# Hybrid retention / HGRN2 decoder step on one core: the HGRN scan of a head spread over two projection units, four plain output chunks, and stores of split weights on the SP queue

## The chip, the cores and the metric

The kernel runs on one core of a Trainium2 chip. A core has TensorE (PE, matrix products; PEld is its weight load), VectorE (DVE), ScalarE (ACT), GpSimd (POOL) and SyncE (SP, here only an issuer of DMAs). The metric is the device time of one execution in microseconds. Three runs of the kernel before gave 1113.52, 1116.01 and 1116.64 us, so the median is 1116.01 us.

## What is computed

One decoder layer for a prompt of 2048 tokens and for 8 single decode tokens, model width 1024. Cut to what matters here:

```python
h = rmsnorm(x, norm_g)
p = h @ w_in                                   # 1024 -> 8 groups of 512 columns
rq, rk, rv, rg, hq, hf, hi, hgate = jnp.split(p, 8, axis=-1)
# retention, 4 heads of 128: rotary on rq and rk, one fixed decay per head
o_ret, s_ret_new = chunked_decay_recurrence(rq, rk, rv, log_gamma, s_ret)
o_ret = head_rmsnorm(o_ret, ret_g) * jax.nn.silu(rg)
# HGRN2, 4 heads of 128: a forget gate per token and channel
logf = jnp.logaddexp(jnp.log(lbf), jnp.log1p(-lbf) + jax.nn.log_sigmoid(hf))
kin = (1.0 - lbf) * jax.nn.sigmoid(-hf)
o_hg, s_hg_new = chunked_decay_recurrence(silu(hq), kin, hi, logf, s_hg)
o_hg = head_rmsnorm(o_hg, hg_g) * jax.nn.silu(hgate)
y = x + jnp.concatenate([o_ret, o_hg], axis=-1) @ w_out
y = rmsnorm(y, final_norm_g)
# where S_t = diag(f_t) S_{t-1} + k_t v_t^T  and  o_t = S_t^T q_t
```

Large products are done in three passes: each fp32 operand is split into a high part h (an ACT copy into the matmul's type) and a low part l (a DVE subtraction), and hh + hl + lh is summed.

## The kernel before

**Token stage.** The prompt is cut in 8 pairs of 128-token chunks. Three sets of weights are run over the 8 pairs (24 steps, `v_pair(i, after)`): values and HGRN inputs, then rq with rg, then rk with the HGRN gate. A pair is one step of a Strassen scheme with 7 products of 12 matmuls (tiles `pv{i}a`, `b`, `c`); `after[n]` holds what is emitted behind product n, and a half number means the middle of the next product. In the second set the rotated queries are transposed by `q_flip` (L427, `pqt`) and stored. In the third set the retention recurrence runs a chunk at a time beside the products: `r_flip` (`pkt`), `r_score` (`par`, `rA`), `r_update` (`pur`), `r_out` (`por`, `obr`), `r_turn` (`potr`), placed by `r_steps` (L755). New weights are split by `wg_split`, the next pair's tokens by `tok_ops` and `s_split`, at pairs 8 and 16 both at once.

**Units.** Then come 8 units, one for a head of HGRN in one half of the prompt (4 heads, 2 halves). The fill of a unit is its projection: f and q (`pjfh`, `pjqh`, L872), each in segments of four parts of 6 matmuls. In half 0 a segment has 512, 256 or 264 columns, in half 1 always 512. Beside the fill of unit i runs the scan of the head of unit i-1 (`hgrn_rec`, L1005): `scores0` (`pah`, 128 small matmuls), `scores(1)` and `scores(3)` (`plh`, 128 each), `scores3` (`plh`, 48), each of which needs k and q updated by DVE (`kh` L1040, `qth` L1043) and kept by ACT (`kepth` L1050); then the tail: `k0`, `k1` (transposes `pkh`), `u0`, `u1` (states, `puh` and `sth`), `o0`, `o1` (`poh`; ACT squares L969, POOL's power L111 and L112 for `orsh`, DVE `obh`) and `t0`, `t1` (transposes `poth`, L981). `merge` (L1301) sets where each step stands in the fill, by weights that run over one unit.

**The sides of a unit.** Splits of the tokens of the next block (`x_split`), decode steps (`d_load`, `d_mul`, `d_add`, `d_mm` with tile `pd`) and sums of w_out for the last stage (`t_load_raw`, `t_sum`, `t_spool`) are placed at times of `side_at`, counted in units. Weights of half 0 are split on chip (`w_load`) and the parts stored to DRAM (`w_kept`) by POOL, to be loaded again in half 1.

**Output.** With the scan of the last head run `PLAIN` chunks of the output product in plain form (`py`, 48 matmuls a chunk); the other chunks go in pairs by the Strassen scheme (`o_pair`, `po`, 84 matmuls a pair) with operands T1 to T4 loaded by POOL from what `t_spool` stored.

**Order.** The order on PE is that of the program text. On DVE, ACT, POOL and SP a scheduler orders instructions at build time, with `behind` tying some behind what stands before them; every engine then runs its list in order, so an instruction that waits holds all behind it. POOL computes the power of every norm and also issues DMAs; SP issues all other loads and stores.

Of the kernel before, what the change touches and what calls it, by code (L numbers as in the profile page):

```python
# [41 lines left out]
def step_kernel(ctx, tc, a, out):  # L42
# [100 lines left out]
    def w_load():  # L143
        if len(w_ready) < len(want):
# [10 lines left out]
            for t, x in zip(w_ready[-1], w_kept):  # L155
                w_stores.append((x[n], t))

    def w_next(j):
        n = w_used[0]
        assert want[n] == j  # L160
        while len(w_ready) <= n:
            w_load()
        w_used[0] += 1
        while w_stores:
            dst, t = w_stores.pop(0)
            pool.dma_start(dst, t.bitcast(F32))
        return w_ready[n]
# [259 lines left out]
    def q_flip():  # L427
        c, o = q_wait.pop()
# [326 lines left out]
    def r_steps(p):  # L755
# [7 lines left out]
        if p:  # L763
            put(0, lambda: r_load(cb, "g"))
# [4 lines left out]
        if p:  # L769
            put(0.5, lambda: r_turn(ca - 2))  # L770
        if p < N_V:
            put(3, lambda: r_load(ca, "q"), lambda: r_load(ca, "v"))
            put(3.5, lambda: r_flip(ca))
            put(4, lambda: r_load(ca, "g"))
            put(4.5, lambda: r_score(ca), lambda: r_update(ca))
            put(5.5, lambda: r_out(ca), lambda: r_load(ca + 1, "q"), lambda: r_load(ca + 1, "v"))
# [4 lines left out]
    for i in range(2, n_tok):  # L781
        after = {n: [] for n in range(7)}
        m, j = i // N_V + 1, i % N_V
        if N_V <= i < 2 * N_V:
            after[2.5] = [q_flip]
        if N_V < i <= 2 * N_V:
            after.setdefault(0.5 if i < 2 * N_V else 2, []).append(q_flip)
# [10 lines left out]
        elif i + 1 < n_tok:  # L798
# [4 lines left out]
            after[2] += [  # L803
                lambda i=i, t=tied: t(lambda: tok_ops(i + 1)), lambda i=i, t=tied: t(lambda: s_split(i + 1, 0))
            ]
            after[4] += [lambda i=i, t=tied: t(lambda: s_split(i + 1, 1))]
# [20 lines left out]
        if i >= N_V - 1 and j in (7, 0) and i < n_tok - 1:  # L827
            for n, (_, op, _) in enumerate(CHAIN):
                if (n + SPLIT_AT) // 7 == (j + 1) % N_V:
                    after[(n + SPLIT_AT) % 7] += [lambda op=op: behind(lambda: wg_split(op))]  # L830
        if i == n_tok - 1:
            after[0] += [w_load]
            after[1] += [lambda: x_alloc(0), lambda: x_raw.update({(0, kp): x_load(0, kp) for kp in range(4)})]
            for kp in range(4):
                after[3 + kp] += [lambda kp=kp: behind(lambda: x_split(0, kp, x_raw[0, kp]))]
# [16 lines left out]

    SEGS = {
# [4 lines left out]
    def seg_steps(w, half, seg, name, evac):  # L858
# [3 lines left out]
        def step(part):  # L862
            if part == 0:
                box["ps"] = ps_pj.tile([P, n], F32, tag="pj", name=f"pj{name}_{t0}")
# [68 lines left out]
    def tail_steps(half, hd, acol, qcol, vcol, kT, decay, old, eps, gcol, name, ksb, ns):  # L933
        st = pools["up"].tile([P, ns, P], F32, tag=f"st{ns}", name=f"st{name}")
        ob = {}

# [8 lines left out]
        def uu(g):  # L945
            pu = ps_lv.tile([P, 4, P], F32, tag="lv", name=f"pu{name}{g}")
            for j in range(4):
                pe.matmul(pu[:, j], ksb[g][:, j], vcol(4 * g + j), start=True, stop=True)
            for j in range(4):
                c = 4 * g + j  # L950
                dst = st[:, c % ns] if c < CH - 1 else pools["S"][hd - NH]
                src = old if c == 0 else st[:, (c - 1) % ns]
# [5 lines left out]
        def oo(g):  # L958
            po = ps_o.tile([P, 4, P], F32, tag="o", name=f"po{name}{g}")
# [806 lines left out]
```

## Time and profile before

| | before |
|---|---|
| median of three runs | 1116.01 us |
| profiled execution | 1114.73 us |
| its span, first to last instruction | 1113.0 us |
| mean granted TensorE clock | 0.979 |
| PE busy | 1051.3 us (94%) |
| DVE busy | 773.0 us (69%) |
| ACT busy | 555.1 us (50%) |
| POOL busy | 161.3 us (14%) |
| DMA moved | 248.31 MB, mean 223 GB/s |

Stages, from the first matmul of each: token stage 0 to 583 us, the 8 units 583.02 to 919.34, the last head's scan with the plain chunks 919.34 to 964.91, the Strassen output 964.91 to 1106. Busy time of PE counts pipelined matmuls with their overlapping ends, so it is no measure of lost time: a stage is read by its length against that of an undisturbed stage with the same matmuls. PEclk in a row is the granted clock of that stretch, 1.00 at full speed.

### The profile page before, as it was taken

What the parts mean: (1) busy time and instruction counts of PE and PEld (TensorE: products, weight loads), DVE (VectorE), ACT (ScalarE), POOL (GpSimd) and SP (SyncE); (2) the same over time, 40 slices, a digit from 0 to 9 for tenths busy, and PEclk for the clock granted to TensorE, in tenths of its full rate; (3) what the DMA queues carried; (4) which work ended last, traced back from release to release, by engine and by line L of the source; (5) the groups of instructions that cost most, each with busy time, mean ns of one, the idle gap of its engine ahead of it and who ended that gap; (6) DMA issues with size and microseconds to landing.
All of it is one profiled execution on the core that took longest, in us unless ns stands there. A gap on an engine that the chain in (4) does not pass through costs nothing.

```text
span 1113.0 us, 22326 instructions
## 1 busy us (share of the span) xinstructions
PE 1051.3 (94%) x8731; PEld 863.9 (78%) x8731; DVE 773.0 (69%) x1405; ACT 555.1 (50%) x1207; POOL 161.3 (14%) x276
## 2 busy tenths in 40 slices
PE   9999999899999899999998899998899889899997
PEld 7777777788778788888886788786686777678775
DVE  6777765786677866666665667576557688577776
ACT  7853436443436555555555466465445465323232
POOL 1410001000001011111112131120110211512112
PEclk9999999999999999999998899999999999899999
DMA  8688989378679855555555974477547573965652
GB/s 292 197 312 323 332 303 358 141 251 297 221 271 296 283 174 170 168 175 174 182 187 211 359 265 159 131 231 245 178 136 221 156 255 111 282 214 171 227 172 94
DMA packets 145081, 248.31 MB, mean 223 GB/s; under 512 B 10609, under 2 KB 78465, under 8 KB 144721
## 3 DMA queue, kind: packets, MB, share of 16 engines
q1 hardware_dynamic: 129120, 196.17, 53.0%
q0 software_dynamic: 15584, 50.44, 12.5%
q8 instruction: 68, 1.11, 0.4%
q14 instruction: 37, 0.30, 0.1%
q10 hardware_dynamic: 272, 0.30, 0.1%
HBM read 162.32 MB, written 84.54 MB: 222 GB/s over the span
## 4 chain that ended last, share of the span: by engine, by line
PE 68%; DMA 9%; issue 7%; DVE 7%; POOL 4%; ACT 3%; SPq 0%; POOLq 0%; DVEq 0%; ACTq 0%
PE po L332 11%; PE pjfh L872 6%; PE pjqh L872 5%; DMA xn<-in_x_prompt 2%; DMA v_dram<-vo 2%; PE pv L332 2%; DMA rq<-qt_dram 2%; PE par L702 1%; PE por L715 1%; PE pur L709 1%; PE plh L1070 1%; PE por L717 1%; POOL ms L257 1%; PE pv3a L332 1%; PE pv11a L332 1%
## 5 line engine op out<-in xcount | busy, mean ns | idle before, releaser
L872 PE MATMUL pjfh<-xh,w_h 128*128 128x512 f32 (+2 forms) x160 | 63.0, 394 | 0.0
L872 PE MATMUL pjqh<-xh,w_h 128*128 128x512 f32 (+2 forms) x160 | 61.0, 381 | 0.0
L872 PE MATMUL pjfh<-xh,w_l 128*128 128x512 f32 (+2 forms) x160 | 59.3, 370 | 1.7 <-issue 1.7
L872 PE MATMUL pjfh<-xl,w_h 128*128 128x512 f32 (+2 forms) x160 | 59.5, 372 | 0.4 <-DVE xl L116 0.4
L872 PE MATMUL pjqh<-xh,w_l 128*128 128x512 f32 (+2 forms) x160 | 57.2, 358 | 0.0
L872 PE MATMUL pjqh<-xl,w_h 128*128 128x512 f32 (+2 forms) x160 | 57.0, 357 | 0.0
L1050 ACT ACTIVATE kepth<-kh 128x1024 f32<-128x1024 f32 x24 | 25.4, 1060 | 61.8 <-DVE kh L1040 61.7
L1040 DVE TENSOR_TENSOR kh<-kh,fph 128x512 f32<-128x512 f32 x48 | 33.4, 696 | 21.2 <-PE plh L1070 19.0
L731 DVE SCALAR_TENSOR_TENSOR obr<-por,omr,rg 128x128 f32<-128x128 f32 x64 | 18.0, 345 | 37.0 <-POOL omr L729 32.7
L115 ACT ACTIVATE ab_h<-xr 128x512 fp32r<-128x512 f32 (+1 forms) x40 | 32.5, 840 | 17.8 <-DVE xr L286 16.8
L116 DVE TENSOR_TENSOR ab_l<-xr,ab_h 128x512 fp32r<-128x512 f32 (+1 forms) x40 | 37.5, 954 | 4.9 <-ACT ab_h L115 4.9
L872 PEld LDWEIGHTS pjfh<-xh,w_h 128*128 128x128 f32 x160 | 33.3, 208 | 8.8 <-issue 5.1
L969 ACT ACTIVATE jkh<-poh 128x128 f32<-128x128 f32 x64 | 17.9, 279 | 43.4 <-PE poh L965 42.1
L872 PEld LDWEIGHTS pjfh<-xh,w_l 128*128 128x128 f32 x160 | 33.1, 207 | 6.0 <-issue 1.5
L872 PEld LDWEIGHTS pjfh<-xl,w_h 128*128 128x128 f32 x160 | 33.1, 207 | 4.2 <-DVE xl L116 1.0
L872 PEld LDWEIGHTS pjqh<-xh,w_h 128*128 128x128 f32 x160 | 31.0, 194 | 5.5 <-issue 1.6
L872 PEld LDWEIGHTS pjqh<-xh,w_l 128*128 128x128 f32 x160 | 30.8, 193 | 4.5
L974 DVE SCALAR_TENSOR_TENSOR obh<-poh,orsh,v 128x128 f32<-128x128 f32 x64 | 18.1, 345 | 22.3 <-POOL orsh L112 13.7
L872 PEld LDWEIGHTS pjqh<-xl,w_h 128*128 128x128 f32 x160 | 31.1, 194 | 3.3
L286 DVE SCALAR_TENSOR_TENSOR xr<-xr,g_in,rb 128x256 f32<-128x256 f32 x64 | 26.7, 480 | 9.4 <-DMA xr<-in_x_t 4.3
L1563 DVE SCALAR_TENSOR_TENSOR xro<-xro,yms,fg 128x1024 f32<-128x1024 f32 (+1 forms) x15 | 18.1, 1213 | 21.5 <-POOL yms L112 21.5
L1043 DVE TENSOR_TENSOR qth<-qth,fph 128x512 f32<-128x512 f32 x48 | 32.8, 683 | 0.0
(1913 smaller groups left out, 3461.6 us busy)
## 6 DMA issues: line engine op xcount, KB each, us to landing
xr<-a_dram SPq DMA_DIRECT2D x24, 512.0 KB
S<-s_dram SPq DMA_DIRECT2D x24, 512.0 KB
xn<-in_x_prompt SPq DMA_DIRECT2D x32, 256.0 KB
xr<-in_x_t SPq DMA_DIRECT2D x16, 512.0 KB
a_dram<-xr SPq DMA_DIRECT2D x16, 512.0 KB
s_dram<-S SPq DMA_DIRECT2D x16, 512.0 KB
wgr<-in_w SPq DMA_DIRECT2D x16, 512.0 KB
xr<-a_dram SPq DMA_DIRECT2D x32, 256.0 KB
```

The source lines that it names most:

```text
L115: act.activation(h, src, AF.Copy)
L116: dve.tensor_tensor(l, src, h.bitcast(F32), op=ALU.subtract)
L286: dve.scalar_tensor_tensor(r[:, k], r[:, k], g_in[:, kk : kk + 1], spread_to[i], op0=ALU.mult, op1=ALU.mult)
L332: pe.matmul(ps, xx, ww, start=(first and n == 0), stop=(last and n == 2), skip_group_check=more)
L731: dve.scalar_tensor_tensor(o[:, cc], po[:, h], ms[:, h : h + 1], rb_of[c, "g"][:, cc], op0=ALU.mult, op1=ALU.mult)
L872: pe.matmul(ps, ww[:, kk], x[:, k, b0 : b0 + n], start=(k == 0 and i == 0), stop=(k == KT - 1 and i == 2),)
L969: act.activation(jk, po[:, j], AF.Square, accum_out=ms[:, j : j + 1])
L974: dve.scalar_tensor_tensor(ob[g][:, j], po[:, j], rs[:, j : j + 1], gcol(4 * g + j), op0=ALU.mult, op1=ALU.mult)
L1040: dve.tensor_tensor(kv[:, :, 0, :], kv[:, :, 0, :], two[:, :, 1:2].to_broadcast([P, nb, b]), op=ALU.mult)
L1043: dve.tensor_tensor(qv[:, :, 1, :], qv[:, :, 1, :], two[:, :, 0:1].to_broadcast([P, nb, b]), op=ALU.mult)
L1050: act.activation(ss[:, 512:], k[:, :HALF], AF.Copy)
L1563: dve.scalar_tensor_tensor(xro[c][:, cc], xro[c][:, cc], ms[:, 0:1], fg[:, cc], op0=ALU.mult, op1=ALU.mult)
```

## The change

1. **Scan of a head over two units.** `hgrn_rec` gives two lists. The scores and `k0`, `k1` (`levels`) run beside the next unit, at 0.08, 0.3, 0.52, 0.74, 0.93 and 0.96 of its fill; the states, outputs and transposes (`rest`) run beside the unit after that, at 0.02 to 0.7. The decays are copied to a tile of their own (`dec`, one DVE copy of 8 columns a head).
2. **Four plain chunks** in place of two (`PLAIN`): 96 plain matmuls more, one Strassen pair of 84 fewer. The last stage carries the rest of the last but one head and the whole of the last.
3. **DMAs from POOL to SP.** 52 DMAs: the 16 stores of split weights, the 16 stores of w_out sums (`t_store`, apart from the split and later) and the 20 loads of T1 to T4.
4. **Longer first unit.** The first four parts of unit 1 are run in unit 0 (`HEADED`, in a bank of another PSUM pool), and the last chunk of retention is spread over them.
5. **Flips later.** The transposes of rotated queries come one to three products later, oldest first; in pair 16 the retention steps come half a product later and the first `r_out` goes to pair 17; splits at pairs 8 and 16 come later, the splits of the first block of tokens one product earlier.
6. Decode products `d_mm` and the loads for w_out sums get other times.

```diff
+        while w_stores and w_stores[0][0] <= n:
+            _, dst, t = w_stores.pop(0)
+            sp.dma_start(dst, t.bitcast(F32))
...
-        c, o = q_wait.pop()
+        c, o = q_wait.pop(0)
...
+            d = 0 if p else 0.5
+            put(3.5 + d, lambda: r_flip(ca))
...
-            after[2.5] = [q_flip]
+            after[3.5 if i > N_V + 1 else 4.5 if i > N_V else 5.5] = [q_flip]
...
+            late = 2 if same(i) else 0
+            after[2 + late] += [
...
-                after[3 + kp] += [lambda kp=kp: behind(lambda: x_split(0, kp, x_raw[0, kp]))]
+                after[2 + kp] += [lambda kp=kp: behind(lambda: x_split(0, kp, x_raw[0, kp]))]
...
+                pl, tag = (ps_lv, "lv") if name == HEADED and t0 == 0 else (ps_pj, "pj")
...
-        steps = [(1.0, scores0), (2.3, lambda: scores(1)), (0, load), (2.3, lambda: scores(3)), (2.3, scores3)]
...
+        levels = [(0.08, scores0), (0.3, lambda: scores(1)), (0.4, load), (0.52, lambda: scores(3)),
+                  (0.74, scores3), (0.93, t["k0"]), (0.96, t["k1"])]
+        rest = [(0.02, begin), (0.12, t["u0"]), (0.24, t["u1"]), (0.36, t["o0"]), (0.44, t["o1"]),
+                (0.6, t["t0"]), (0.7, t["t1"]), (0.7, last)]
...
+    def t_store(k, n):
+        for x, y in zip("hl", tspl[k, n]):
+            sp.dma_start(t_dram[x, n][:, :, k], y.bitcast(F32).rearrange("p (a b) -> p a b", a=2))
...
-        merge(fill, rec)
-        rec = hgrn_rec(*order[i], u)
+        merge(fill, levels, late)
+        late = rest
+        levels, rest = hgrn_rec(*order[i], u)
...
-            pool.dma_start(t, t_dram[x, pair[0]][:, pair[1]])
+            sp.dma_start(t.bitcast(F32), t_dram[x, pair[0]][:, pair[1]])
...
-    PLAIN = 2
+    PLAIN = 4
...
-    merge(fill, rec, 0.95)
+    merge(fill, [(0.57 * at, f) for at, f in levels], [(0.57 * at, f) for at, f in late], [(0.55 + 0.5 * at, f) for at, f in rest])
```

Three places show how rows moved. The names in them: `x_h` and `x_l` are parts of a split operand, a number at the end of a name is a buffer.

On PE, at the scores of head 2 of half 0 (`pah`, in unit 3), before:

```order
L872 MATMUL pjfh_0_6920<-xh_5157,w_l 128x512
L1089 MATMUL pah_6936<-qh_6521,kh_6520 32x32 x32
L1070 MATMUL pah_6936<-qth_6522,kh_6520 32x16 x32
L872 MATMUL pjfh_0_6920<-xh_5157,w_h 128x512
L872 MATMUL pjfh_0_6920<-xl_5158,w_h 128x512
```

and after:

```order
L879 MATMUL pjfh_0_6858<-xh_5116,w_l 128x512
L1104 MATMUL pah_6874<-qh_6391,kh_6390 32x32 x32
L1085 MATMUL pah_6874<-qth_6392,kh_6390 32x16 x32
L960 MATMUL puh_6959<-v_6542,ksh_6830 128x128 x4
L879 MATMUL pjfh_0_6858<-xh_5116,w_h 128x512
L879 MATMUL pjfh_0_6858<-xl_5117,w_h 128x512
```

The states `puh` of the head before now follow the first scores. From `pah` to the next burst of scores (`plh`) stood 12 projection matmuls; now 18 stand there and both groups of `puh`. On the whole the four bursts of a unit are 22% of its fill apart, where they were 14%.

On POOL, at the norm of the head before the last (`orsh`, in unit 7), before, with loads of operand T2 among them:

```order
L1424 DMA oT2l_9990<-t_draml_5378 128x512
L111 TENSOR_SCALAR orsh_9673<-omsh_9664 128x4
L112 TENSOR_TENSOR orsh_9673<-orsh_9673,mhalf 128x4
L1424 DMA oT2l_9991<-t_draml_5378 128x512
L1424 DMA oT2l_9992<-t_draml_5378 128x512
L111 TENSOR_SCALAR orsh_9699<-omsh_9690 128x4
L112 TENSOR_TENSOR orsh_9699<-orsh_9699,mhalf 128x4
```

and after, at the norm in the same unit:

```order
L1157 DMA out_new_hgrn_prompt<-S_5579 128x128
L111 TENSOR_SCALAR orsh_9369<-omsh_9360 128x4
L112 TENSOR_TENSOR orsh_9369<-orsh_9369,mhalf 128x4
L111 TENSOR_SCALAR orsh_9417<-omsh_9408 128x4
L112 TENSOR_TENSOR orsh_9417<-orsh_9417,mhalf 128x4
```

No DMA stands between the two norms any more. The loads stand on SP, in the same unit, among loads of w_out (`wor`) and of outputs (`or`):

```order
L1453 DMA oT2h_10264<-t_dramh_5376 128x512
L1240 DMA out_new_hgrn_sample<-dS_9117 128x8x128
L1392 DMA wor_9624<-in_w_out 128x1024
L1453 DMA oT2h_10265<-t_dramh_5376 128x512
L1453 DMA oT2h_10266<-t_dramh_5376 128x512
L1392 DMA wor_9647<-in_w_out 128x1024
L1481 DMA or_9670<-o_dram 128x8x128
L1481 DMA or_9676<-o_dram 128x8x128
```

A load of T2 that waits for its buffer now holds the loads of `wor` and `or` behind it.

115 lines of the change are left out of this document (62 added, 53 removed).

## The prediction

> **What bounds the kernel now.** I read the page first, then the granted clock and busy time by stretch, the waits of PE, and the timeline at the longest of them.
>
> ```profile
> span 1113.0 us, 22326 instructions
> PE 1051.3 (94%) x8731; PEld 863.9 (78%) x8731; DVE 773.0 (69%) x1405; ACT 555.1 (50%) x1207; POOL 161.3 (14%) x276
> q1 hardware_dynamic: 129120, 196.17, 53.0%
> q0 software_dynamic: 15584, 50.44, 12.5%
> q8 instruction: 68, 1.11, 0.4%
> ```
>
> PE is the bound, but 94% hides how much it loses, because overlapping matmuls count as busy. So I compare stretches with equal work. The next fence has one row for unit 0, one for each of units 1 to 7, and one for the last head's scan with the plain chunks; its columns are the length, the busy time of PE, PEld, DVE, ACT and POOL with their instructions, the granted clock (PEclk), the DMA share and GB/s.
>
> ```profile
> 583.02:621.34 38.32, 33.42 (x189) 28.85 (x188) 21.57 (x45) 19.34 (x51) 7.30 (x12) 0.87 0.70 245
> 621.34:666.93 45.59, 39.97 (x641) 35.45 (x639) 31.55 (x68) 24.99 (x54) 12.11 (x18) 0.93 0.86 309
> 666.93:703.71 36.78, 36.25 (x640) 32.53 (x640) 26.59 (x64) 23.18 (x52) 8.79 (x14) 1.00 0.43 161
> 703.71:747.13 43.42, 38.60 (x639) 33.90 (x640) 27.79 (x55) 24.86 (x54) 7.26 (x10) 0.94 0.55 175
> 747.13:790.83 43.70, 39.43 (x600) 31.68 (x600) 29.38 (x66) 23.00 (x48) 3.01 (x6) 0.94 0.70 224
> 790.83:834.46 43.63, 39.35 (x609) 30.84 (x610) 24.80 (x53) 19.80 (x45) 4.08 (x7) 0.96 0.52 158
> 834.46:877.34 42.88, 39.05 (x617) 30.54 (x618) 29.08 (x57) 20.08 (x46) 5.80 (x10) 1.00 0.76 228
> 877.34:919.34 42.00, 37.84 (x610) 30.24 (x610) 33.86 (x61) 25.64 (x51) 6.35 (x11) 1.00 0.59 191
> 919.34:964.91 45.57, 39.12 (x594) 31.34 (x594) 32.46 (x58) 23.78 (x52) 13.20 (x24) 0.92 0.55 166
> ```
>
> Unit 2 (666.93) took 36.78 us at full clock; the others, with nearly the same matmuls, took 42.0 to 45.6. No engine is full in them (DVE at most 33.86 of 42.00). So a unit costs 36.8 us and the rest is waiting. Units 4 to 7 also hold 1, 2, 3 and 2 decode products. The timeline of PE (start, length, work, and in brackets the idle time before it) prices them at 0.57 us each (855.01 to 855.58), and four small products of 128 columns at 0.38 (198.33 to 198.71).
>
> ```profile
> 194.80 0.39 PE L332 MATMUL pv8c<-T1h,s71l 128*128 128x512 f32 x1
> 198.33 0.63 PE L431 MATMUL pqt<-ident,vo 128*128 128x128 f32 x4 [3.13 <-DVE vo L354]
> 198.71 0.48 PE L332 MATMUL pv8c<-T1h,s71h 128*128 128x512 f32 x1
> ...
> 855.01 0.64 PE L563 MATMUL pd<-dS,dqp 128*32 128x256 f32 x8
> 855.58 0.50 PE L872 MATMUL pjqh<-xh,w_h 128*128 128x512 f32 x1
> ```
>
> Loss in unit 1 is then 8.8; in units 2 to 7 it is 0, 6.6, 6.3, 5.7, 4.4 and 4.0, together 27.0. For unit 0 and the last stretch I need prices of long matmuls, from the chain of waits, where a run of PE without a wait stands as one piece (start, length, count):
>
> ```profile
> 667.17 2.79 PE pjfh L872 x12
> ...
> 675.36 3.02 PE pjfh L872 x24
> ...
> 679.66 3.11 PE pjfh L872 x24
> ...
> 1072.68 32.92 PE po L332 x144
> ```
>
> They give 0.2325 us for 512 columns, 0.126 and 0.130 for 256 and 264, 0.2286 in the output stage. The fill of unit 2 is 48 of each of the first three, 23.4 us, so the scan of a head is 13.4 us of PE. Unit 0 has that fill and 44 small products, 4.2 us: it loses 10.7. The last stretch has 96 x 0.2286 = 21.9 and one scan: it loses 10.3. **From 583 to 965 us, 57 us are lost**, and these are where the change works.
>
> What they are lost to, by the waits of PE (total, times, longest) and the places:
>
> ```profile
> PE poth L981 <- DVE obh L974: 12.8, 10, 2.3
> PE plh L1070 <- issue: 8.4, 4, 3.3
> PE plh L1070 <- ACT kepth L1051: 5.0, 3, 3.9
> PE potr L740 <- DVE obr L731: 4.5, 2, 2.5
> PE pqt L431 <- DVE vo L354: 3.1, 1, 3.1
> PE pjfh L872 <- issue: 1.7, 2, 1.1
> ...
> PE pkt L694 <- DVE rk L354: 1.6, 1, 1.6
> PE por L715 <- DVE rA L704: 1.7, 1, 1.7
> ```
>
> A wait is dear, since the clock falls behind it: after the 3.1 us before `pqt`, the stretch of this row (columns as above) ran at 0.51 for 3.5 us, which costs 1.7 more.
>
> ```profile
> 199.50:203.00 3.50, 3.50 (x10) 2.73 (x9) 3.50 (x4) 2.12 (x4) 0.00 (x0) 0.51 0.64 186
> ```
>
> The timelines of PE, DVE and POOL at four waits:
>
> ```profile
> 587.95 1.15 PE L740 MATMUL potr<-ident,obr 128*128 128x128 f32 x4 [1.97 <-DVE obr L731]
> ...
> 628.24 1.22 DVE L116 TENSOR_TENSOR w_l<-wr,w_h 128x1024 fp32r<-128x1024 f32 x1 [3.41 <-ACT w_h L115]
> ...
> 711.45 0.39 PE L1070 MATMUL plh<-qth,kh 128*32 128x16 f32 x25
> 713.95 0.51 PE L1070 MATMUL plh<-qth,kh 128*32 128x16 f32 x37 [2.12 <-issue]
> ...
> 916.13 0.53 POOL L1424 DMA_DIRECT2D oT2l<-t_draml  x1 [0.99 <-DVE obh L974]
> 916.73 0.19 POOL L111 TENSOR_SCALAR orsh<-omsh 128x4 f32<-128x4 f32 x1
> ```
>
> At 711.45 PE stops in the middle of a burst with nothing awaited. The 17462 PE instructions over 68 packets of the instruction queue are 257 a packet of 16 KB, so I read this as PE's next block of program not yet there: a burst of 128 small matmuls with their loads is a whole block, and two bursts stood 12 matmuls (2.8 us) apart. At 628.24 DVE stood 3.41 us for a weight that had not landed, and the scan's updates behind it. At 916.13 POOL held the norm behind a load of T2 that waited for `obh`.
>
> **The change, part by part.**
>
> *Scan over two units.* No matmul is added; a copy of 8 columns a head is nothing on DVE. The output chain (ACT squares, POOL, DVE `obh`) before `poth` had an eighth of a fill, 2.9 us, and gets 24 to 26%, 5.6 us and more; its longest wait was 2.3, so all ten should go. The bursts get 22% of 23.4, 5.1 us, and 0.8 of `puh`, 5.9 in place of 14%, 3.3. The wait at 713.95 was 2.1, so it is covered, unless a block ends just at a burst's start; then spacing does not help. DVE, ACT and POOL do the same work in fewer us: unit 7 has 33.86 us of DVE in some 38, 89%. So I leave in units 2 to 7 one stall like 713.95 with its slow clock (2.1 + 1.7) for every two units, 11 us, and take 27.0 - 11 = **-16.0**. Bounds: nothing gained, or all 27.0.
>
> *Unit 1.* The fourth weight is asked for ahead of the eight loads of values instead of behind four of them, and the first burst gets 12 x 0.126 + 24 x 0.130 = 4.6 us in place of 2.8. But DMA was 0.86 busy there, and with no rest beside it the later bursts stay close. Half: **-4.4**, between 0 and -8.8.
>
> *Unit 0.* The first `potr` stands behind the same matmuls, so its 2.0 and the slow clock stay. The second gets 24 matmuls where it had 6, 4.2 us more against its 2.5: the wait goes, and the slow clock that followed, of which I count 3.4 us (the row's 0.87 of 38.32 is 5.0 us in all, less 1.7 for the first). Against it, the parts of the next block are now split closer to their use: four DVE subtractions of 1.2 (the length at 628.24) against six matmuls of 0.126 each, a new wait of 1.2. **-4.7**, between 0 and -9.
>
> *Last stretch.* 192 plain matmuls stand beside one and a half scans. DVE gets two more chunks, and each chunk must leave its bank before the next but one; I halve the loss: **-5.2**, between +2 (a DVE wait of 2.3, as the longest of `poth`, at three chunk ends, with the old loss kept in part) and -10.3. The stage as a whole does 96 matmuls more and 84 fewer: 12 x 0.2286 = **+2.7**, on PE for certain.
>
> *Flips.* `pqt` of pair 8 comes three products, 36 matmuls or 8.2 us, later against a wait of 3.1; wait and slow clock go, **-4.8**. `pkt` and `por` of pair 16 wait 3.3; DVE is behind there, and the move of half a product (1.4) and of `r_out` should take most: **-2.0**, between 0 and -3.3.
>
> *52 DMAs from POOL to SP.* On POOL, a store or load before a norm goes (916.13); its gain is in the `poth` row already. On SP the stores wait for a split that PE needs at the same time, so I cost them at nothing; what hides them is that weights are loaded a whole unit ahead. If that cover is gone, each late weight costs what unit 1 shows, below. They are 24 MB (16 + 16 of 0.5, 16 of 0.25, 4 of 1) of q0's 50.44 MB: q1 gets them.
>
> A rule that speaks against this: the Trainium skill, "DMA: Bandwidth & Descriptors", section "Queues, rings and completion order", says each DMA engine takes turns between the queues that have work, a packet at a time. By that the 24 MB had turns of their own on q0 and would now stand in line with the loads on q1; the sum would get the price of the slow rival below.
>
> Another: "Runtime: NRT & Kernel Launch", section "Instruction fetch mechanics", in the Trainium skill, calls the cost of crossing a block of 256 instructions mostly hidden. The 257 a packet agree with the block; the 2.12 at 713.95 does not look hidden. By the rule the issue waits would have another cause, spacing would not touch them, and the sum would be that of the first rival.
>
> Sum: -16.0 - 4.4 - 4.7 - 5.2 + 2.7 - 4.8 - 2.0 = -34.4. The profiled execution took 1114.73 us, 1.3 below the median 1116.01, so 1114.7 - 34.4 = **1080 us**.
>
> **Rivals.** *The bursts still starve.* If issue waits come from DMA traffic alone, spacing gains nothing: the 10.1 us of the two issue rows stay, with the slow clock of units 3 to 5 (0.94, 0.94, 0.96 of some 43.5: 6.9) and the 4.4 of unit 1, less some 6 of the 11 already left: +15, **1095**. For it: DMA moved 160 to 309 GB/s in these units. Against: unit 6, at 228 GB/s, kept a clock of 1.00.
>
> *Nearly all goes.* If units 2 to 7 keep 1 us each (6 for 11), units 1 and the last stretch 2 each (4 for 9.5), pair 16 nothing (for 1.3) and unit 0 only its first wait with the slow clock (3.7 for 6.0), it is 14 less: **1066**. Against: DVE at 89%.
>
> *Slower: weights late on SP.* SP works in order, and a store that waits for its split, or a load of T2 or T1 that waits for its buffer, holds the next weight. Unit 1 gives the price of one late weight: 8.8 us. Half 0 has 8 weights, half 1 loads 8 again. With four late, all the 34 are gone; with six, it is 1080 + 53 = **1133**. For it: DMA 0.86 busy in unit 1, where most stores fall. Against: weights are needed about every 18 us.
>
> **How the numbers follow.** My forecast, 1071 to 1089, has 0.50; starving bursts 0.22; nearly all gone 0.16; late weights 0.12, of which 0.02 end within 0.3% (3.3 us, about what a measurement of this kernel can tell from no change) and 0.10 above. So faster 0.88, same 0.02, slower 0.10. The range takes the forecast and the larger part of both neighbours: 1060 to 1100.
>
> **What would show it.** `poth` should leave the list of waits; units 2 to 7 should take 37 to 40 us each at a clock of 0.97 or more; `pqt` should have no wait and 199 to 203 no slow clock; the last stretch should take 43.9 + 20 + 5 = 69 us. I am wrong if a group of `w_h` or `w_l` on a DMA, or new waits of PE for DVE, take more than 10 us in the units, or if waits of `plh` on issue stay above 8 us.

## The result and the profile after

The changed kernel took 1087.61 us, the median of four runs (1085.89 to 1091.66), against 1116.33 for the kernel before in the same session: a ratio of 0.975, 95% interval 0.9715 to 0.9784. The profiled execution took 1087.88 us, 26.9 less than the 1114.73 of before; the forecast was 34.4 less.

The head of the page, engines and queues:

```profile
span 1086.1 us, 22296 instructions
PE 1043.2 (96%) x8743; PEld 860.5 (79%) x8743; DVE 760.8 (70%) x1400; ACT 553.3 (51%) x1204; POOL 127.9 (12%) x224
...
q1 hardware_dynamic: 139424, 221.34, 61.5%
q0 software_dynamic: 7328, 25.27, 6.6%
q8 instruction: 69, 1.13, 0.4%
```

POOL lost its 52 DMAs (276 to 224 instructions), and q0's 50.44 MB became 25.27. The waits of PE (total, times, longest):

```profile
PE plh L1085 <- issue: 10.7, 4, 4.1
PE pkt L694 <- DVE rk L354: 3.1, 2, 2.2
PE prs L273 <- DVE dg L268: 2.5, 2, 2.1
...
PE plh L1130 <- issue: 1.9, 1, 1.9
...
PE pqt L431 <- DVE vo L354: 0.3, 1, 0.3
```

`poth` (12.8 before) and `potr` (4.5) are gone, and `pqt` fell from 3.1 to 0.3. Stops on issue inside the score bursts (`plh`) did not fall: 10.7 and 1.9, together 12.6, against 8.4 before. With the stops at other matmuls PE stood 13.0 us on issue, against 10.1 before.

The stretches, from one head's `pah` to the next, then the one behind `pqt` (length, busy time of PE, PEld, DVE, ACT and POOL, granted clock, DMA share, GB/s). The first row is unit 0, the second unit 1 without its first four parts, then units 2 to 7 and the beginning of the last stretch:

```profile
579.92:618.11 38.19, 35.62 (x226) 31.25 (x224) 19.21 (x44) 18.95 (x47) 4.83 (x7) 1.00 0.70 234
618.11:650.74 32.63, 27.60 (x562) 24.26 (x561) 26.43 (x53) 19.72 (x34) 0.00 (x0) 0.95 0.86 301
650.74:691.26 40.52, 37.95 (x639) 33.88 (x638) 30.07 (x69) 25.93 (x55) 3.61 (x6) 0.96 0.66 223
691.26:735.00 43.74, 37.74 (x640) 33.91 (x639) 27.12 (x64) 23.19 (x52) 3.59 (x6) 0.96 0.78 248
735.00:773.31 38.31, 36.49 (x600) 30.07 (x599) 27.28 (x56) 22.72 (x48) 4.33 (x6) 1.00 0.70 204
773.31:810.16 36.85, 36.85 (x607) 30.09 (x606) 24.25 (x52) 19.15 (x45) 3.59 (x6) 1.00 0.75 217
810.16:849.07 38.91, 38.34 (x618) 30.74 (x617) 28.89 (x57) 19.77 (x46) 5.78 (x7) 1.00 0.64 200
849.07:890.05 40.98, 38.62 (x609) 31.46 (x608) 33.67 (x61) 27.46 (x54) 6.48 (x9) 0.96 0.62 194
890.05:923.00 32.95, 28.64 (x510) 24.14 (x510) 23.42 (x46) 13.47 (x32) 4.92 (x9) 0.90 0.43 136
...
199.50:203.00 3.50, 3.50 (x19) 2.68 (x18) 3.47 (x5) 3.33 (x7) 0.00 (x0) 1.00 0.32 120
```

Unit 5 (773.31) has two decode products of 0.57, so an undisturbed unit of half 1 is 35.7 us. That agrees with its fill, 96 x 0.2325 = 22.3 in place of 23.4.

To compare stages whose borders moved, I priced every matmul at the interval that follows it in undisturbed runs (0.227 us for 512 columns, 0.118 and 0.121 for 256 and 264, 0.0143 for a small score) and summed what lies above. A slow clock is in these losses too:

| stage | lost before | lost after | change | forecast |
|---|---|---|---|---|
| 186 to 215 us (`pqt` of pair 8) | 6.5 | 2.2 | -4.3 | -4.8 |
| 354 to 383 us (pair 16) | 4.1 | 2.0 | -2.1 | -2.0 |
| rest of the token stage | 17.0 | 20.0 | +3.0 | 0 |
| unit 0 | 11.2 | 4.1 | -7.1 | -4.7 |
| unit 1 | 9.3 | 6.4 | -2.9 | -4.4 |
| units 2 to 7 | 32.7 | 18.9 | -13.8 | -16.0 |
| last scans and output | 11.6 | 9.1 | -2.5 | -5.2 |
| 12 more matmuls | | | +2.7 | +2.7 |
| sum | | | -27.0 | -34.4 |

The longest waits left in the units have one cause. The timeline of PE in unit 3, then the DMA of the 6.6 us ahead of the fetch of the next block of program, and of the 1.2 us that hold it (packets, MB, share of 16 engines):

```profile
699.40 0.65 PE L1085 MATMUL plh<-qth,kh 128*32 128x16 f32 x56
704.19 0.30 PE L1085 MATMUL plh<-qth,kh 128*32 128x16 f32 x6 [4.14 <-issue]
```

```profile
q1 hardware_dynamic: 620, 2.17, 90.5%
q14 instruction: 1, 0.01, 0.5%
```

```profile
q1 hardware_dynamic: 128, 0.40, 93.5%
q8 instruction: 1, 0.02, 6.1%
```

PE stopped at 700.05 with six matmuls of the burst to go. Until 701.7 the engines were 90% busy with q1 and no block of PE's program (q8, 16 KB) came; one came then, and PE went on at 704.19. A block is about 256 instructions (17622 records of PE, weight loads included, over 69 packets), so its borders can be placed by counting these records in the order of their start. In the traces of both kernels and of the twelve versions below there are 68 stops on issue of 0.6 us or more. Each stands 193 or 194 records past a multiple of 256, whatever the matmul is there, and at each PE goes on 1.2 to 1.6 us after the last packet of q8 has ended. So these stops are borders of blocks that came late.

In the units of the changed kernel a packet starts 0.9 to 1.1 us after PE enters the block before the one it brings where the DMA engines stand idle, and mostly 1.5 to 5 us, at most 7.6, after where they are busy. A block that is one burst lasts 1.2 us; in the long matmuls of the token stage a block lasts 20 us and more, and there no stop of this kind occurs. The experiments test the border and the traffic.

### The profile page after: what moved, and what is told of

The parts are those of the page before. It is cut to its first block, busy times and chain, and to the rows that moved or that the text cites. A ratio compares the mean times of both kernels' runs of the same rounds, so it can differ in the third digit from the quotient of the medians.

```text
span 1086.1 us, 22296 instructions
## 1 busy us (share of the span) xinstructions
PE 1043.2 (96%) x8743; PEld 860.5 (79%) x8743; DVE 760.8 (70%) x1400; ACT 553.3 (51%) x1204; POOL 127.9 (12%) x224
## 2 busy tenths in 40 slices
DMA packets 147130, 248.34 MB, mean 229 GB/s; under 512 B 10608, under 2 KB 78464, under 8 KB 146768
## 3 DMA queue, kind: packets, MB, share of 16 engines
q0 software_dynamic: 7328, 25.27, 6.6%
q8 instruction: 69, 1.13, 0.4%
## 4 chain that ended last, share of the span: by engine, by line
PE 65%; DMA 13%; DVE 8%; ACT 7%; issue 4%; POOL 2%; SPq 1%; DVEq 0%; POOLq 0%; ACTq 0%
PE po L332 11%; PE pjfh L879 5%; PE pjqh L879 5%; DMA xn<-in_x_prompt 4%; PE py L1502 4%; DMA qt_dram<-qt 2%; PE par L702 1%; PE plh L1085 1%; PE pur L709 1%; PE por L715 1%; PE puh L960 1%; DMA wr<-in_w_in 1%; PE poh L976 1%; PE por L717 1%; DMA wg1B<-in_w 1%
## 5 line engine op out<-in xcount | busy, mean ns | idle before, releaser
L879 PE MATMUL pjfh<-xh,w_h 128*128 128x512 f32 (+2 forms) x160 | 59.9, 374 | 0.0
L879 PE MATMUL pjfh<-xh,w_l 128*128 128x512 f32 (+2 forms) x160 | 57.0, 356 | 0.7 <-DVE w_l L116 0.7
L879 PE MATMUL pjfh<-xl,w_h 128*128 128x512 f32 (+2 forms) x160 | 57.2, 357 | 0.4 <-DVE xl L116 0.3
L1065 ACT ACTIVATE kepth<-kh 128x1024 f32<-128x1024 f32 x24 | 25.4, 1060 | 62.0 <-DVE kh L1055 58.2
L115 ACT ACTIVATE ab_h<-xr 128x512 fp32r<-128x512 f32 (+1 forms) x40 | 32.3, 840 | 17.1 <-DVE xr L286 17.0
L879 PEld LDWEIGHTS pjfh<-xh,w_l 128*128 128x128 f32 x160 | 30.8, 192 | 5.9 <-DVE w_l L116 1.6
L879 PEld LDWEIGHTS pjfh<-xh,w_h 128*128 128x128 f32 x160 | 30.6, 191 | 5.5 <-issue 1.2
L879 PEld LDWEIGHTS pjfh<-xl,w_h 128*128 128x128 f32 x160 | 30.8, 193 | 4.3 <-DVE xl L116 1.0
L742 ACT ACTIVATE obr<-potr,pk 128x128 f32<-128x128 f32 x64 | 19.0, 368 | 21.7 <-PE potr L740 21.7
L1592 DVE SCALAR_TENSOR_TENSOR xro<-xro,yms,fg 128x1024 f32<-128x1024 f32 (+1 forms) x13 | 15.5, 1202 | 18.5 <-POOL yms L112 18.5
```

The lines of the kernel that those rows point to most:

```text
L115: act.activation(h, src, AF.Copy)
L742: act.activation(o[:, cc], pt[:, h], AF.Copy, scale=ng[:, h : h + 1])
L879: pe.matmul(ps, ww[:, kk], x[:, k, b0 : b0 + n], start=(k == 0 and i == 0), stop=(k == KT - 1 and i == 2),)
L1065: act.activation(ss[:, 512:], k[:, :HALF], AF.Copy)
```

## The experiments

Each is the changed kernel but for its diff, of which the main lines are shown; the last two stand on half bursts. "The changed kernel" is 1087.61 us, ratio 0.975 (0.9715 to 0.9784); every ratio is to the kernel before, run beside it.

**The scan back in one unit.**

```diff
-        merge(fill, levels, late)
-        late = rest
+        merge(fill, levels, rest)
...
-        levels = [(0.08, scores0), (0.3, lambda: scores(1)), (0.4, load), (0.52, lambda: scores(3)),
+        levels = [(0.063, scores0), (0.207, lambda: scores(1)), (0.207, load), (0.352, lambda: scores(3)),
...
-    merge(fill, [(0.57 * at, f) for at, f in levels], [(0.57 * at, f) for at, f in late], [(0.55 + 0.5 * at, f) for at, f in rest])
+    merge(fill, levels, rest)
```

> The changed kernel with one part undone: the states, outputs and transposes of a head's scan stand again in the unit of its scores, at the places of the kernel before; all else is as changed. Theory (the spread is what brought the gain in the units): units 1 to 7 and the last stretch lose again what they lost before, less what the other parts saved, 14 to 20 us more than the changed kernel's 1087.6, so 1102 to 1108, and waits of poth on obh come back with 8 us or more. Rival (the gain in the units came from the stores on SP and the later side work): within 4 us of 1087.6, and poth below 3 us.

1104.88 us, ratio 0.9911 (0.988 to 0.9943): 17.3 us slower. Units 2 to 7 lost 36.0 in place of 18.9, unit 1 11.8 in place of 6.4, the last stage 2.6 less than the changed kernel. The waits of PE:

```profile
PE poth L994 <- DVE obh L987: 10.5, 8, 4.3
PE plh L1085 <- issue: 10.0, 8, 2.3
```

The waits of `poth` came back, as the first theory had it. The stops on issue in `plh` are about as long as with the spread, in more and shorter pieces. With 4.3 us at `pjfh` they are 15.2 us in all against 13.0: the spread did little for them.

**All 52 DMAs on POOL again.**

```diff
-            sp.dma_start(dst, t.bitcast(F32))
+            pool.dma_start(dst, t.bitcast(F32))
...
-            sp.dma_start(t.bitcast(F32), t_dram[x, pair[0]][:, pair[1]])
+            pool.dma_start(t.bitcast(F32), t_dram[x, pair[0]][:, pair[1]])
```

> The changed kernel with the 52 DMAs issued by POOL again, at their new places in the program. Theory (their queue is worth nothing to PE): within 3 us of 1087.6; POOL busy about 160 us in place of 128, q0 at 50 MB. Rival 1 (the DMAs on POOL hold the norms behind them): 5 to 8 us slower, with waits on orsh or of poth on obh of 5 us or more. Rival 2 (stores with turns of their own let the loads through): 4 us or more faster, because stalls of plh on issue or waits of DVE for weights shrink. A rule of the Trainium skill, 'DMA: Bandwidth & Descriptors', section 'Queues, rings and completion order', that a DMA engine takes turns between its queues, would give rival 2.

1103.59 us, ratio 0.990 (0.9871 to 0.9929): 16.0 us slower, more than either of the first two had it. The traced execution, 1097.68 us, is the fastest of nine; it began unit 0 4.3 us earlier than that of the changed kernel. In it the last stage lost 20.1 in place of 9.1, at one place. The wait of PE, and the timeline of POOL there:

```profile
PE poth L994 <- DVE obh L987: 9.1, 1, 9.1
```

```profile
949.14 0.39 POOL L111 TENSOR_SCALAR orsh<-omsh 128x4 f32<-128x4 f32 x1
958.34 0.81 POOL L1447 DMA_DIRECT2D woh<-t_dramh  x1 [8.82 <-issue]
959.18 1.04 POOL L112 TENSOR_TENSOR orsh<-orsh,mhalf 128x4 f32<-128x4 f32 x1
```

The second of two loads of T4 into the tiles of w_out stood 8.8 us on POOL between the two halves of one norm; DVE's `obh` and then PE's `poth` stood behind it. What the load waited for the profile does not show (`<-issue`); the load of `wol` ahead of it, issued at 948.29, took 9.7 us to land, that is until 958.0.

**Only the 32 stores on POOL**, the loads of T1 to T4 on SP.

```diff
-            sp.dma_start(dst, t.bitcast(F32))
+            pool.dma_start(dst, t.bitcast(F32))
...
-            sp.dma_start(t_dram[x, n][:, :, k], y.bitcast(F32).rearrange("p (a b) -> p a b", a=2))
+            pool.dma_start(t_dram[x, n][:, :, k], y.bitcast(F32).rearrange("p (a b) -> p a b", a=2))
```

> The changed kernel with the 32 stores issued by POOL again, the 20 loads of T1 to T4 left on SP. Theory (of the 16 us that all 52 on POOL cost, a load of T2 or T4 that waits for its buffer held the norm of the last head, 9 us at one place; stores wait for nothing long): within 4 us of 1087.6, and no wait of poth on obh above 2 us. Rival (the stores hold norms too, one by one): 5 to 10 us slower, without a long wait in the last stretch. A third way (stores with turns of their own let weights through, the rule on queues of the Trainium skill, 'DMA: Bandwidth & Descriptors', section 'Queues, rings and completion order'): 4 us or more faster.

1093.22 us, ratio 0.979 (0.9767 to 0.9813), 5.6 us slower by the medians, with intervals that overlap. No wait of `poth` remained, and the last stage lost 8.9. So by the medians about 10 of the 16 us are the 20 loads, through the norm above. For the rest there is the trace of the slowest of the four (1097.91 us): units 1 and 3 lost 11.2 and 13.8 in place of 6.4 and 7.3, by waits for `qth`, `fxh` and `w_l` and slower clocks; which store causes them stays open. The third way, a gain from queues that take turns, did not come.

**Flips back.**

```diff
-        c, o = q_wait.pop(0)
+        c, o = q_wait.pop()
...
-            after[3.5 if i > N_V + 1 else 4.5 if i > N_V else 5.5] = [q_flip]
+            after[2.5] = [q_flip]
...
-            after.setdefault(2.5 if i < N_V + 3 else 1.5 if i < 2 * N_V else 2, []).append(q_flip)
+            after.setdefault(0.5 if i < 2 * N_V else 2, []).append(q_flip)
```

> The changed kernel with the transposes of rotated queries at their old places and latest first; the retention steps of pair 16 stay as changed. Theory (the prediction's term of 4.8): the wait of pqt comes back with some 3 us at pair 8, the stretch of 29 us there loses 4 us more, and the time is 3 to 6 us above the changed kernel's 1087.6. Rival (the wait only moves: DVE is behind there and the split of the next pair's tokens takes its place): the stretch loses within 1 us of the 2.2 it loses now, and the time within 2 us.

1091.71 us, ratio 0.9784 (0.9763 to 0.9804): 4.1 slower by the medians, with intervals that overlap. The wait of PE and the stretch behind it, which is the row of before once more:

```profile
PE pqt L431 <- DVE vo L354: 4.6, 3, 3.7
```

```profile
199.50:203.00 3.50, 3.50 (x10) 2.80 (x9) 1.40 (x2) 1.09 (x2) 0.00 (x0) 0.50 0.51 142
```

From 186 to 215 us 7.4 were lost in place of 2.2. The term of 4.8 is borne out in this stretch, slow clock included.

**Two plain chunks.**

```diff
-    PLAIN = 4
+    PLAIN = 2
```

> The changed kernel with two plain chunks instead of four beside the last scans. Theory (the prediction's balance of 2.7 more matmul time against 5.2 less loss): the matmuls of the stage take 2.7 us less, but one and a half scans stand beside half as many fills, bursts and the output chain of the last head have no cover, and the stage loses 8 us or more over the changed kernel's 8.4; the time is 3 to 10 us above 1087.6. Rival (the tail spreads as well over two chunks): 1 to 4 us faster than the changed kernel, the 2.7 us of matmuls saved.

1091.70 us, ratio 0.9792 (0.9754 to 0.983): 4.1 slower by the medians, with intervals that overlap. The last stage lost 16.6 in place of 9.1, 7.5 more, with waits of `plh` for `sth` (3.2) and `poth` for `obh` (2.8); less the 2.7 of matmuls that makes 4.8. By this trace four chunks are worth it because the spread scan needs a cover there.

**The first unit as before.**

```diff
-    HEADED = "fh01"
+    HEADED = None
...
-            next_unit = unit(1)
-            early += [f for w, f in next_unit[0][:4]]
-            del next_unit[0][:4]
...
-                if n in (0, 1, 3, 5, 7, 11):
+                if n in (0, 1, 2, 4, 6, 7):
```

> The changed kernel without the longer first unit: the first four parts of unit 1 stand in unit 1 again, and the last chunk of retention is spread over 8 parts. Theory (the prediction's term of 4.7 for unit 0, read as 7 from the trace of the changed kernel): a second wait of 2 us or more for obr or rk in unit 0 comes back with a slow clock, unit 0 and unit 1 together lose 3 to 7 us more than the 10.5 they lose now, time 1090 to 1095. Rival (unit 1, the busiest for DMA, is eased when it keeps its four parts): what unit 0 loses unit 1 gains, the time within 3 us of 1087.6.

1088.23 us, ratio 0.9749 (0.9705 to 0.9792): no difference. Unit 0 lost 7.4 in place of 4.1, with a wait of `potr` for `obr` of 2.4, and unit 1 lost 4.0 in place of 6.4, as the rival had it. The longer unit moves a loss of 3 us from one unit to the next.

**Bursts cut in two.**

```diff
-        def scores(li):
-            pl = ps_lv.tile([P, 2, CH, 16], F32, tag="lv", name=f"pl{name}{li}")
+        def scoresa(li):
+            pl = box["pl"] = ps_lv.tile([P, 2, CH, 16], F32, tag="lv", name=f"pl{name}{li}")
             small(pl[:, 0], li, box["kept"])
+
+        def scores(li):
+            pl = box["pl"]
             small(pl[:, 1], li + 1)
...
+        levels = [(0.08, scores0a), (0.13, scores0), (0.3, lambda: scoresa(1)), (0.36, lambda: scores(1)), (0.4, load),
+                  (0.53, lambda: scoresa(3)), (0.59, lambda: scores(3)), (0.76, scores3),
```

> The changed kernel with each burst of 128 score matmuls cut in two of 64, a step of 6 projection matmuls or more between them; the same matmuls. Theory (PE outruns the fetch of its program, one block of 256 instructions ahead, and the fetch waits behind DMA traffic): a block then lasts longer at the bursts, and the waits on issue of plh, 12.6 us in the changed kernel, fall to 3 to 8; the time falls by 3 to 9 us, to 1079 to 1085. Rival (the fetch waits so long behind traffic that a few us more a block don't help): issue waits stay between 10 and 15 and the time within 3 us of 1087.6.

1084.37 us, ratio 0.9726 (0.9679 to 0.9773): 3.2 less by the medians, which the intervals do not tell from the changed kernel. The stops halved:

```profile
PE plh L1085 <- issue: 6.1, 3, 3.2
PE plh L1142 <- DVE qth L1058: 3.4, 1, 3.4
...
PE plh L1137 <- ACT kepth L1066: 3.1, 1, 3.1
```

Two new waits in unit 1, for DVE's update of `qth` and ACT's copy `kepth`, which now have less room, took back half of it: the unit lost 9.8 in place of 6.4.

**Less DMA traffic: no stores of split weights**, each weight read whole and split again in half 1.

```diff
-            if n >= 2 * NH:
+            if False:
...
-                w_stores.append((n, x[n], t))
+                pass
```

> The changed kernel without the 16 stores of split weights; in half 1 each weight is loaded whole once more (0.5 MB in place of two parts of 0.5 MB) and split again on ACT and DVE. 8 MB of stores leave units 0 to 3, 4 MB of loads leave units 4 to 7; DVE gets 8 subtractions of 1.2 us in units 4 to 7. Theory (fetches wait behind DMA traffic): fetches in units 0 to 3 start sooner, stalls on issue there (about 12 us of loss at 625, 635, 638, 660 and 700) halve, and the time falls by 3 to 8 us, to 1080 to 1085. Rival (the stores lie in gaps of the traffic, and DVE is the tighter engine): no fewer stalls on issue, new waits for w_l in half 1, 1088 to 1095.

1092.98 us, ratio 0.982 (0.9771 to 0.9869): 5.4 slower by the medians, with intervals that overlap a little. The traced execution, 1087.62 us, is the fastest of the four; it began unit 0 4.9 us earlier than that of the changed kernel and lost that again. DMA moved 235.74 MB in place of 248.34, and yet the stops on issue that were 10.7 are 13.0, and unit 3 lost 11.8 in place of 7.3. So fewer bytes on the whole did not help; the theory in that form fell. What stayed the same is the place. The timeline of PE with its stop, here and with the 32 stores on POOL, two programs with other traffic and the same order on PE as the changed kernel:

```profile
695.68 0.30 PE L1085 MATMUL plh<-qth,kh 128*32 128x16 f32 x6 [5.50 <-issue]
```

```profile
711.10 0.30 PE L1085 MATMUL plh<-qth,kh 128*32 128x16 f32 x6 [4.01 <-issue]
```

Three times PE stops with six of the burst to go. That fits the border of a block, and just as well a fault of the burst itself. The next two runs separate these.

**64 matmuls more in the warm-up.**

```diff
-    for n in range(14):
-        pe.matmul(wu, ones, ones, start=True, stop=True)
+    for n in range(14 + 64):
+        pe.matmul(wu[:, :16] if n > 13 else wu, ones, ones[:, :16] if n > 13 else ones, start=True, stop=True)
```

> The changed kernel with 64 matmuls of 16 columns more in the warm-up at the start, 128 instructions or half a block of program, while PE still waits for its first operands; nothing else is changed. Theory (PE stops where a block of its program ends while a fetch waits behind traffic): the stops on issue move to other matmuls or change in length by 1 us or more each, and their sum lies between 6 and 18 us against 12.6; the time lies within 5 us of 1087.6. Rival (the stops come from the bursts themselves, a bank of PSUM or an operand): the same bursts stop at the same matmul for the same time, within 0.5 us.

1111.2 us, ratio 0.9962 (0.9942 to 0.9983): 23.6 slower, outside both. The groups of instructions on PE show why (busy, mean ns of one):

```profile
L84 PE MATMUL wu<-ones 128*128 128x16 f32 x128 | 24.9, 352 | 0.0
L84 PE MATMUL wu<-ones 128*128 128x128 f32 x28 | 5.6, 391 | 1.1 <-POOL ones L78 1.1
```

The first product of the token stage began at 31.33 us in place of 6.96: the added work was on the path. And such a matmul stands twice in the trace (64 as 128, as 14 stand as 28), with its weight load each time: 256 instructions, a whole block (the page has 70 packets of instructions in place of 69). So the borders of blocks did not move in the program, and the stops stayed: 4.1 us in unit 3 and 3.8 in the last stretch, where the changed kernel has 4.3 and 3.8 by the same pricing. The five stops of over 1 us in the changed kernel stand at the same matmuls again, with 20, 10, 6, 7 and 21 of their burst to go. The run tells the theories apart no further.

**Half a block more, behind unit 0.** The first head's first scores do one group twice.

```diff
             small(p0, 0)
+            if half == 0 and "n" not in pools:
+                pools["n"] = small(p0, 0)
             update(0)
```

> The changed kernel with one group of 64 small matmuls of the first scores (first head of half 0) done twice, into the same bank: 128 instructions, half a block, and under 1 us more before everything behind it; the warm-up is left alone. Theory (PE stops where a block ends while the next is not fetched): behind that place blocks end half a block earlier in the program, so the stops on issue of units 2 and 3 and of the last stretch (2.0, 4.3 and 3.8 us in the changed kernel) come at other matmuls of the burst, at least two of the three differ by 1 us or more in length, and the time lies 0 to 8 us off 1087.6 on either side. Rival (the stops belong to the burst: a bank, an operand or the clock): each of the three stops stands at the same matmul of its burst with the same length within 0.5 us, as they did with a whole block more.

1082.75 us, ratio 0.9709 (0.9673 to 0.9745): 4.9 less than the changed kernel by the medians, with more work and intervals that overlap a little. In the changed kernel the stops of unit 2 and of the last stretch, beside the one at 704.19, are these:

```profile
661.95 0.27 PE L1085 MATMUL plh<-qth,kh 128*32 128x16 f32 x10 [1.84 <-issue]
...
904.53 0.51 PE L1085 MATMUL plh<-qth,kh 128*32 128x16 f32 x21 [3.65 <-issue]
```

With the shift, units 1 to 4 and the stretch behind the last `pah`, then stops in bursts of units 1 and 4:

```profile
614.18:651.61 37.43, 28.38 (x626) 25.20 (x625) 28.84 (x59) 20.51 (x35) 0.00 (x0) 0.95 0.81 288
651.61:688.18 36.57, 36.09 (x639) 32.39 (x638) 27.80 (x63) 24.85 (x54) 3.61 (x6) 1.00 0.63 220
688.18:726.16 37.98, 36.34 (x639) 32.74 (x638) 27.13 (x64) 23.21 (x52) 3.60 (x6) 1.00 0.87 286
726.16:771.01 44.85, 38.35 (x600) 31.52 (x599) 27.33 (x56) 22.88 (x48) 5.39 (x6) 0.96 0.57 174
888.75:921.70 32.95, 32.28 (x575) 27.06 (x575) 27.06 (x53) 17.57 (x42) 6.07 (x11) 1.00 0.48 151
```

```profile
625.38 0.32 PE L1085 MATMUL plh<-qth,kh 128*32 128x16 f32 x15 [2.04 <-issue]
...
632.62 0.46 PE L1085 MATMUL plh<-qth,kh 128*32 128x16 f32 x34 [1.65 <-issue]
...
727.90 0.49 PE L1085 MATMUL pah<-qth,kh 128*32 128x16 f32 x35 [0.75 <-issue]
...
752.79 0.24 PE L1085 MATMUL plh<-qth,kh 128*32 128x16 f32 x4 [3.62 <-issue]
```

Unit 2 took 36.57 us and unit 3 37.98, in place of 40.52 and 43.74: their stops of 2.0 and 4.3 (by the pricing above) are gone, and so is the 3.8 of the last stretch, whose clock here is 1.00 where it was 0.90 and whose loss fell from 9.1 to 3.3. But in unit 4, whose longest stop was 1.0, one of 3.6 appeared, and the unit took 44.85 us in place of 38.31; unit 1 has stops of 2.0, 1.7 and 1.3 where it had one of 1.9. DMA was busier in unit 3 than in the changed kernel (0.87, 0.78). So the same bursts beside as much traffic stop or don't by where the program's blocks end.

The stops moved more than they shrank: PE stood 11.6 us on issue in all, against 13.0. Units 1 to 7 together took 274.57 us (614.18 to 888.75), against 271.94 (618.11 to 890.05) in the changed kernel. Of the 7.1 us by which the traced span is shorter, 5.8 lie in the last stretch and the output, and 3.9 ahead of the added group, where every engine runs the same instructions in the same order; 2.6 were lost in the units between. How much of the 4.9 the shift is worth stays open.

**Half bursts, w_out sums moved**, in two ways.

```diff
-    for k, at in enumerate((0.4, 1.0, 1.8, 2.5)):
+    for k, at in enumerate((0.4, 1.0, 1.8, 4.45)):
```

> The kernel with half bursts, and the fourth group of w_out sums (its loads, sums and 2 MB of stores) moved from units 2 and 3 to units 4 and 5, away from the ten loads of the next block of tokens. Theory (fetches wait behind the traffic of that place): the stop in the scores of unit 3, 4.3 us in the changed kernel and 2.5 with half bursts, falls under 1 us, unit 3 loses 2 to 4 us less, and the time is 1078 to 1083. Rival (what holds the fetch is the loads of tokens, whatever else runs): the stop stays above 2 us, and the time is that of half bursts, 1084.4, or more, since units 4 and 5 get the work.

1083.31 us, ratio 0.9705 (0.9683 to 0.9726), 4.3 under the changed kernel by the medians, with intervals that overlap a little. The stop of unit 3 went: the unit lost 0.2 in place of 7.3, and stops on issue of `plh` fell to 2.9. Half bursts alone, with the same order on PE and so the same borders, lost 4.3 there, so the traffic of that place does matter. Unit 5 lost 3.2 in place of 0.1, by a wait for `kept` (2.1).

```diff
-    for k, at in enumerate((0.4, 1.0, 1.8, 2.5)):
+    for k, at in enumerate((0.4, 1.4, 2.2, 3.7)):
```

> Half bursts with the second, third and fourth group of w_out sums moved to where no late update and no load of tokens stands beside them (1.4, 2.2 and 3.7 in place of 1.0, 1.8 and 2.5). Theory: unit 1 loses 4 to 7 us in place of 9.8 with half bursts, unit 3 under 2 in place of 4.3, and the time is 1075 to 1081, below both kernels. Rival (the waits of DVE in unit 1 come from weights that land late, not from the sums): unit 1 loses 9 or more still, and the time is 1081 to 1086, as with the other half-burst kernels.

1088.04 us, ratio 0.9765 (0.9726 to 0.9804): neither. Unit 1 lost 4.8 in place of 9.8 with half bursts, as the theory had it, but one wait in unit 4 took it back. The waits of PE, and the issues of SP ahead of it:

```profile
PE pjqh L879 <- DMA w_h<-w_kepth: 9.4, 1, 9.4
```

```profile
729.31 0.52 SPq L1210 DMA_DIRECT2D t_dramh<-wos30h  x1
...
732.50 0.51 SPq L1210 DMA_DIRECT2D t_draml<-wos31l  x1
...
734.19 2.02 SPq L179 DMA_DIRECT2D xr<-a_dram  x2
736.32 1.14 SPq L149 DMA_DIRECT2D w_h<-w_kepth  x1
```

The four stores waited 5.2 us on SP for their splits ahead of the weight, which was then asked for at 736.32, and PE stood 9.4 us for it. They were not alone: ahead of them SP had waited 6.4 us for DVE with a load of tokens, and 2.1 with one of a decode state.

## Why the prediction was right, and where it was off

The forecast was faster, 1080 us in 1060 to 1100; it was faster, 1087.6.

*Scan over two units (-16.0).* Right in mechanism and close in size: -13.8, and +17.1 in these units when undone. `poth` left the list, as said. The part on the bursts failed: "so it is covered" did not hold for stops like that at 713.95: in all, those in the scores came to 12.6, more than the 8.4 before. The exception that stood beside it, "unless a block ends just at a burst's start", named the right variable, and it turned out to be the rule and not the exception: four of the five stops of over 1 us came with 6 to 21 of a burst's 128 matmuls to go, so that most of such a burst was one block. Of units 2 to 7 three took the 37 to 40 us that were forecast or less (38.3, 36.9, 38.9), three more (40.5, 43.7, 41.0).

*Undisturbed unit (36.8).* Too high by 1.1 for half 1, whose fill is smaller; 4 to 5 us of loss in units 4 to 7 were overlooked.

*Unit 1 (-4.4) and unit 0 (-4.7).* Together -10.0 against -9.1. The reason given for unit 0, more matmuls ahead of the second `potr`, is right for that wait (2.4 when undone), but the longer unit as a whole is worth 0.6 us, since unit 1 pays. Unit 1's gain hangs on the spread (5.4 of loss came back without it), and also on the stores (4.8 with them on POOL). The step "its 2.0 and the slow clock stay" failed: the first wait of `potr` went too, and though PE waited 2.2 us for `rk` in this unit (`pkt`), the row's clock is 1.00. So the slow clock that was priced behind a wait does not follow every wait. What else eased unit 0 was not tried alone.

*Last stretch (-5.2) and 12 matmuls (+2.7).* -2.5, and the stretch took 70.8 us where 69 were forecast. The step "I halve the loss" was too kind by one stop on issue, 3.8 us, which is not there with half a block of shift.

*Flips (-4.8, -2.0).* -4.3 and -2.1, and 4.1 when the first was undone. The rest of the token stage came out at +3.0. The waits of `prs` for `dg` are not the reason: they took 2.7 before and 2.5 after. Versions with the same order up to unit 0 begin it at times 3.8 us apart (last section), so the +3.0 can't be told from chance.

*52 DMAs from POOL to SP (0).* The step that failed most, though it cost the forecast nothing. "Its gain is in the `poth` row already" took two causes of one wait for one term. With the scan spread and the loads left on POOL, 16.0 us are lost, 9.1 of them in one wait of `poth`; with the loads moved and no spread, 17.3. Each part is needed, and what they bring alone does not add up.

*The rivals.* "The bursts still starve" (1095) was half right: the stops stayed, above the 8 us that I named as a sign of being wrong, but the terms of unit 0, the flips and `poth` came in. 1087.6 lies midway. Its cause, traffic alone, is not what the runs show: traffic sets how late a block comes, the border of the block sets whether a burst waits for it. "Late weights" did not occur in the changed kernel; its price of 8.8 us a weight was met by the 9.4 us of the last run.

*Rules of the Trainium skill.* "Runtime: NRT & Kernel Launch", section "Instruction fetch mechanics", of the Trainium skill calls the crossing of a block mostly hidden. The 4.14 us in mid burst, gone from there with half a block of shift, disagree for bursts beside full DMA engines; in the matmul stretches of the token and output stages the runs agree, since none of the 68 stops is there. The turns between queues of "DMA: Bandwidth & Descriptors", section "Queues, rings and completion order", of the Trainium skill would have made the move of the stores a loss; the kernel with the stores on POOL was 5.6 us slower, so no run here shows it at work.

**Versions below both kernels by their medians:** half a block of shift (1082.75) and half bursts with the fourth sums in unit 4 (1083.31). All eight runs of the two lie under the fastest of the changed kernel (1085.89). They were not tried together.

## What to carry to other kernels

A DMA that may wait does not belong on an engine's queue between two instructions of a chain that the critical engine waits for; look for that wait in the schedule you will have, not in the one you profile. Where PE stops on issue inside a run of small matmuls, spread them through the long ones: with half bursts all waits of PE on issue fell from 13.0 to 6.5 us, and to 3.3 with less traffic beside them. A shift of the program by half a block moves such stops; here they were 11.6 us after it. Two changes that remove the same wait are one term, and each can be worth all of it when the other is there.

## What was not expected of the hardware

The 32 added small matmuls (64 in the trace) moved every stop behind them, and with more work the kernel was 4.9 us faster by the medians. Not all of that need be the shift. That version and six others above run the same instructions in the same order up to unit 0 as the changed kernel, and yet begin it between 576.94 and 580.78 us, where the changed kernel began it at 579.92. Differences of 4 us between two versions of this kernel may be such chance, and some of those above (half bursts, stores on POOL, flips back, two plain chunks) can't be told from it.

In the warm-up run PE was busy without a gap from 1.13 to 31.33 us, and the granted clock still fell to half. The stretches of that run:

```profile
13.00:24.00 11.00, 11.00 (x53) 11.00 (x53) 5.34 (x14) 6.65 (x18) 0.00 (x0) 0.50 0.87 320
...
30.00:36.00 6.00, 6.00 (x18) 5.03 (x19) 0.00 (x0) 0.00 (x0) 0.00 (x0) 0.50 0.00 0
```

Matmuls of 16 columns, each with a load of 128 weights, did not hold the clock: in these rows it is 0.50, and it stayed so until the long products had run for 5 us.
